# Second layer of a decoder step: keys' transposes a chunk later, values' products of four units in one visit, sums of squares later

## The chip, the cores and the metric

The kernel runs on one core of a Trainium2 chip. The metric is the device time of one execution in microseconds (us). The core has five engines with a queue each: TensorE (PE, matrix products and transposes; its loading of weights is shown apart as PEld), VectorE (DVE), ScalarE (ACT), GpSimd (POOL) and SyncE (SP, which mostly issues DMAs). An engine works through its queue in order; semaphores order the engines among each other.

## The reference

A decoder step of two layers for 1024 prompt tokens and 8 decode tokens, model width 1024. The first layer (retention) is untouched here. The second is attention in a sliding window with 16 query heads, 2 key and value heads, 64 elements a head:

```python
h = rmsnorm(x, g_norm)
q, k, v, gate = jnp.split(h @ w_in, [...], axis=-1)
q = rmsnorm(q.reshape(...), q_gain)              # over the 64 elements of a head
k = rmsnorm(k.reshape(...), k_gain)
# prompt: a block of 128 queries reads its own and the previous block of keys
scores = einsum('bnqkgd,bnskd->bnkgqs', qb, kk) * HD ** -0.5 - slope * dist   # masked
p = softmax(concat([scores, sink]))[..., :-1]
o = einsum('bnkgqs,bnskd->bnqkgd', p, vv)
# decode tokens: the same over the cached 128 keys and values and their own
return x + (o * silu(gate)) @ w_out, k[:, -128:], v[:, -128:]
```

## The kernel before

The text is about the second layer only, which runs from about 885 us to the end. Activations (`A_hi`, `A_lo`) and weights (`wh`, `wl`) are held as a rounded part and a remainder, and a product is made as three: hi·hi, lo·hi and hi·lo. Tokens lie in nine chunks c: eight of 128 prompt tokens and one of the 8 decode tokens; the projections take them in three groups ti of 384, 384 and 264 tokens.

**Keys and values.** A loop over n, 0 to 8. `kv_mm(n, 0)` and `kv_mm(n, 1)` are 12 products each of 256 columns (L1339 to L1341; the decode tokens' are L1336 and L1337). The PSUM tile comes from pool `pjp` (tiles `pj`) for even n and from `scp` (tiles `sc`, two banks) for odd n. `kv_ev` then has ACT write the values `vv` (L1346) and square the keys (L1312, tile `kj`, sums in `kss`), DVE scale the sums (L1313), POOL take the power −1/2 (L115, `krk`), DVE multiply by the token's factor (L1319) and write the normed keys `kd` (L1321). `kv_tr` transposes `kd` on TensorE (L100, `tr`); `kv_kk` splits the transposed keys into `kkh` (ACT, L1365) and `kkl` (DVE, L1366). Between them stand `rbcast`, three products with the unit matrix on DVE (L1396, tile `sq`), and `rbcast_mm`, a product with ones on TensorE (L1403, into an `sc` bank) that ACT copies to `rbc` (L1404): this brings the tokens' factors to all partitions for the gates. `q_conv` and `g_conv` split weights on ACT (L1102) and POOL (L1103) in the same loop. In this block (`sk`) TensorE, ACT, DVE, POOL and SP all keep the written order.

**Projections of queries and gates.** A generator (`pair_proj`, pairs p of heads 0 to 7) makes six tiles a pair: q for the three groups, and the gates g. A tile is 8 steps k of three products (L1132 to L1134). `q_ev` squares on ACT (L1450) and splits the queries; `ms_mm` sums the squares over a head with small products (L1471, L1473), and gives DVE and POOL the factor `rq`. The table `mms` says after which step k of which tile this stands. The generator runs at most four groups ahead of the scores and three ahead of the outputs.

**Units.** A unit is a pair p and a chunk c, 64 in all. `att_s` makes its scores (L1562, L1563, into an `sc` bank), DVE scales them and adds the bias (L1565), takes the maximum (L1567), ACT the exponential (L1569); `att_r` divides (DVE L1576, POOL L1577); `att_x` transposes the four quarters (L100) and ACT copies them to `ptf` (L1587); `att_o` multiplies by the values (L1600, 4 products, 2 for c = 0), ACT takes the result out (L1602), POOL multiplies by the gate (L1603). The main loop m gives, for each unit, the scores of m + 4, projections, the transposes of m + 1, projections, and the values' products of m; `fill(ps, W)` pulls projections of about 0.95 us. From m = 59 on the output projection fills in (`so_all`, generator `out`); `so_ahead` loads its weights and splits them (ACT L1119, DVE or POOL L1122). The decode tokens' scores (`dec_scores`, L1635 and L1640 on TensorE, L1623 to L1645 mostly on DVE) stand at m = 58.

In the main loop TensorE alone keeps the written order; the other engines' orders are set by the scheduler.

Of the kernel before, what the change touches and what calls it, by code (L numbers as in the profile page):

```python
# [7 lines left out]
F32 = mybir.dt.float32  # L8
# [62 lines left out]
def _trunk(ctx, tc, nc, a):  # L71
# [20 lines left out]
    mm = nc.tensor.matmul  # L92
# [501 lines left out]
    o = lambda fn, *a: (fn, a)  # L594
# [25 lines left out]
    n = 0  # L620
# [647 lines left out]
    o = 0  # L1268
# [58 lines left out]
    def kv_mm(c, h):  # L1327

        if h == 0:
            kvst[c] = (pjp.tile([128, 512], F32, tag="pj", name="pj") if c % 2 == 0 else  # L1330
                       scp.tile([128, 512], F32, tag="sc", name="sc"))
        ps = kvst[c]
        cs = slice(c * 128, c * 128 + 128)
        for k in range(4 * h, 4 * h + 4):
            if c == 8:
                mm(ps[0:40, :256], xdec2[:, k, :], kvs[0][:, k, :], start=(k == 0), stop=False)  # L1336
                mm(ps[0:40, :256], xdec2[:, k, :], kvs[1][:, k, :], start=False, stop=(k == 7))  # L1337
            else:
# [15 lines left out]
    def kv_tr(c):  # L1354
        kd = kvst.pop(c)
        pt = kvst["t", c] = trp.tile([128, 512], F32, name="tr")
        for g in range(2):
            tr(pt[:, g * 128:g * 128 + 128], kd[:, g].rearrange("p a b -> p (a b)"), ident)
        if c == 7:
            nc.scalar.dma_start(out=nkp[0, 0], in_=kd[:, :, 0, :])  # L1360

    def kv_kk(c):
        cs = slice(c * 128, c * 128 + 128)
        pt = kvst.pop(("t", c))[:, 0:256].rearrange("p (g t) -> p g t", g=2)
        nc.scalar.activation(kkh[:, :, cs], pt, AF.Copy)  # L1365
        nc.vector.tensor_tensor(kkl[:, :, cs], pt, kkh.bitcast(F32)[:, :, cs], ALU.subtract)  # L1366
# [20 lines left out]
    def rbcast(ti):  # L1387
        t0, t1 = TG[ti]
        n = t1 - t0
        dg = io("sq", 2)  # L1390
        if ti == 2:
            nc.gpsimd.memset(dg[:, 256:264], 0.0)
        for i in range(3):
            c = t0 // 128 + i
            m = 128 if c < 8 else ND
            nc.vector.tensor_scalar(dg[:m, i * 128:i * 128 + m], ident[:m, :m], r9[:m, c:c + 1], None, ALU.mult)  # L1396
        return dg

    def rbcast_mm(ti, dg):
        t0, t1 = TG[ti]  # L1400
        n = t1 - t0
        ps = scp.tile([128, 512], F32, tag="sc", name="sc")
        mm(ps[:, :n], ones, dg[:, :n], start=True, stop=True)  # L1403
        nc.scalar.activation(rbc[:, t0:t1], ps[:, :n], AF.Copy)  # L1404
# [29 lines left out]
    def pair_proj(p):  # L1434
# [64 lines left out]
            G[p, ti] = gt  # L1499

        order = ("q0", "q1", "g0", "q2", "g1", "g2") if p == 7 else ("q0", "q1", "q2", "g0", "g1", "g2")
        mms = {(1, 3): 0, (2, 3): 1, (4 if p == 7 else 3, 3): 2}
        for step, (kind, ti) in enumerate(order):
            ti = int(ti)
            isq = kind == "q"
# [73 lines left out]
    def att_x(u):  # L1579
        hs = (0, 1) if u.c > 0 else (1,)  # L1580
        pt = trp.tile([128, 512], F32, name="tr")
        for hf in hs:
            for j in range(2):
                tr(pt[:, hf * 256 + j * 128:hf * 256 + j * 128 + 128], u.st[:, j, hf * 128:hf * 128 + 128], ident)
        a0 = hs[0] * 256
        ptf = u.pt = atp.tile([128, 512], F32, name="ptf", bufs=2)
        nc.scalar.activation(ptf[:, a0:], pt[:, a0:], AF.Copy)  # L1587

    def att_o(u):
        p, ti, i, c = u.p, u.ti, u.i, u.c  # L1590
        if i == 0:
            ots[p, ti] = atp.tile([128, 384], F32, name="ot", bufs=2)
        ot, gt = ots[p, ti], G[p, ti]
        hs = (0, 1) if c > 0 else (1,)
        po = opp.tile([128, 128], F32, tag="o", name="o")
        vs = slice(u.g * 64, u.g * 64 + 64)
        for hf in hs:
            for j in range(2):
                rs_ = slice(hf * 256 + j * 128, hf * 256 + j * 128 + 128)
                mm(po[j * 64:j * 64 + 64, :], vv[:, c - 1 + hf, vs], u.pt[:, rs_], start=(hf == hs[0]), stop=(hf == 1))  # L1600
        cs = slice(i * 128, i * 128 + 128)
        nc.scalar.activation(ot[:, cs], po, AF.Copy, scale=0.5)  # L1602
        nc.gpsimd.tensor_tensor(ot[:, cs], ot[:, cs], gt[:, cs], ALU.mult)  # L1603
# [188 lines left out]
    def until(d, key):  # L1792
        while key not in d:
            next(ps)
# [7 lines left out]
    dgs = {}  # L1802
    for n in range(9):
        kv_mm(n, 0)
        if n == 2:
            rstd9(1)
        if n >= 2:
            kv_tr(n - 2)
        if 5 <= n < 8:
            rbcast_mm(n - 5, dgs.pop(n - 5))  # L1810
        kv_mm(n, 1)
        if n >= 3:
            kv_kk(n - 3)
        if n >= 1:
            kv_ev(n - 1)
        if 4 <= n < 7:
            dgs[n - 4] = rbcast(n - 4)
        if 1 <= n <= 4:
            q_conv(n - 1)
        if n == 3:  # L1820
            slots["g"], g_load, g_conv = wslot_parts(w_in_swa[:, 1280:1536])
            g_load(0)
        if n == 5:
            g_load(1)
        if 5 <= n <= 8:
            g_conv(n - 5)
    dec_load()
    fill(ps, 2.0)
    kv_kk(6)
    kv_dec()  # L1830
    kv_tr(7)
# [22 lines left out]
    fill(ps, 3.0)  # L1854
    att_r(units[3])
    att_x(units[0])
    sk.close()
    src = ps

# [4 lines left out]
            att_s(u)  # L1864
            att_r(u)

    for m in range(NU):
        u = units[m]
        if m == 50:
            lo_eng[0] = nc.vector  # L1870
            so_ahead(1)
        if m == 56:
            drain(ps)
            so_ahead(2)
        if m == 59:
            so_ahead(3)
            src = out
        reloads(m)
        sc_(m + L)
        if m == 58:  # L1880
            dec_scores()
            dec_vload()
        fill(src, W)
        if m + 1 < NU:
            att_x(units[m + 1])
        if m == 62:
            dec_pt()
        fill(src, W)
        until(G, (u.p, u.ti))
        att_o(u)  # L1890
        reloads(m)
        if m == 63:
            dec_o()
        fill(src, W)
    reloads(NU)
    drain(out)

# [37 lines left out]
```

## Time and profile before

| | |
|---|---|
| time of three runs, median (lowest to highest) | 1350.39 us (1350.27 to 1351.85) |
| the profiled execution | 1350.44 us, span 1348.6 us |
| mean granted clock of TensorE | 0.995 |
| busy: PE, DVE, ACT, POOL | 1308.8, 701.1, 633.6, 707.4 us |
| keys and values stage | 888.9 to 928.8 us, transposes of chunk 7 at 931.5 |
| steady loop over the units | about 1020 to 1225 us |
| scores of units 60 to 63 | from 1226.4 to 1235.2 us |

A row of a timeline reads: start, duration, engine, line of the kernel, operation, output tile <- input tiles, shape, how many records it joins, and in brackets the idle time of that engine just before, with what ended it. Buffer numbers are left out of names. One product of 32-bit numbers leaves two records in some shapes. A window gives the busy time of each engine in it and the granted clock of TensorE (1.00 is full).

### The profile page before, as it was taken

How to read it: one execution, taken by the hardware profiler on the slowest of the kernel's cores; microseconds unless marked ns; L12 is line 12 of the kernel's file. 1: busy time of each engine (PE TensorE's matmuls, PEld its weight loads, DVE VectorE, ACT ScalarE, POOL GpSimd, SP SyncE). 2: the span in 40 equal slices, each digit the busy share in tenths (PEclk: the TensorE clock that was granted, in tenths of full speed). 3: DMA queues.
4: the chain of work that ended last, by engine and by line, in shares of the span. 5: the costliest groups of instructions: out<-in, count | busy, mean ns of one | idle time of the engine just before them, and what ended most of it. 6: DMA issues, size and time to landing. Idle time of an engine off the chain costs nothing.

```text
span 1348.6 us, 25951 instructions
## 1 busy us (share of the span) xinstructions
PE 1308.8 (97%) x9661; PEld 1222.4 (91%) x9661; DVE 701.1 (52%) x1365; ACT 633.6 (47%) x1565; POOL 707.4 (52%) x825
## 2 busy tenths in 40 slices
PE   6999999999999999899999999998999999999998
PEld 6999999999999999787877899997889999998998
DVE  6943655656566553676752113335456555669321
ACT  5532444544455553677751112235465656656321
POOL 6653534435435543698977545454375666555000
PEclk9999999999999999999999999999999999999999
DMA  6314777587676753556556434442121111113532
GB/s 221 103 55 140 218 222 225 161 242 233 187 237 187 233 177 107 169 171 212 182 160 196 153 121 136 143 119 72 38 62 44 48 46 46 34 34 107 159 86 80
DMA packets 194771, 187.68 MB, mean 139 GB/s; under 512 B 12645, under 2 KB 174493, under 8 KB 194629
## 3 DMA queue, kind: packets, MB, share of 16 engines
q1 hardware_dynamic: 156576, 147.29, 35.9%
q10 hardware_dynamic: 38068, 38.73, 9.1%
q8 instruction: 76, 1.25, 0.4%
q14 instruction: 51, 0.41, 0.1%
HBM read 129.61 MB, written 57.41 MB: 139 GB/s over the span
## 4 chain that ended last, share of the span: by engine, by line
PE 85%; DVE 5%; POOL 4%; issue 3%; DMA 2%; ACT 1%; ACTq 0%; SPq 0%; POOLq 0%; DVEq 0%
PE b L330 7%; PE b L332 7%; PE b L331 7%; PE pj L1132 7%; PE pj L1134 6%; PE pj L1133 6%; PE b L323 4%; PE b L324 4%; PE b L325 4%; PE tr L100 4%; PE pj L1181 4%; PE pj L1179 4%; PE pj L1180 4%; PE o L1600 2%; POOL wl L1122 1%
## 5 line engine op out<-in xcount | busy, mean ns | idle before, releaser
L330 PE MATMUL b<-xh,woh 128*128 128x258 f32 x784 | 223.3, 285 | 0.0
L332 PE MATMUL b<-xh,wol 128*128 128x258 f32 x784 | 221.6, 283 | 0.0
L331 PE MATMUL b<-xl,woh 128*128 128x258 f32 x784 | 221.2, 282 | 0.0
L1132 PE MATMUL pj<-A_hi,wh 128*128 128x384 f32 (+1 forms) x512 | 178.7, 349 | 0.0
L1134 PE MATMUL pj<-A_hi,wl 128*128 128x384 f32 (+1 forms) x512 | 165.2, 323 | 0.0
L1133 PE MATMUL pj<-A_lo,wh 128*128 128x384 f32 (+1 forms) x512 | 165.1, 323 | 0.0
L330 PEld LDWEIGHTS b<-xh,woh 128*128 128x128 f32 x784 | 148.0, 189 | 4.1 <-issue 2.5
L331 PEld LDWEIGHTS b<-xl,woh 128*128 128x128 f32 x784 | 148.8, 190 | 0.0
L332 PEld LDWEIGHTS b<-xh,wol 128*128 128x128 f32 x784 | 148.1, 189 | 0.0
L221 POOL TENSOR_TENSOR wol<-raw,woh 128x512 fp32r<-128x512 f32 x52 | 68.5, 1325 | 139.7 <-ACT woh L216 139.0
L1122 POOL TENSOR_TENSOR wl<-wr,wh 128x1024 fp32r<-128x1024 f32 (+1 forms) x60 | 114.2, 1913 | 40.2 <-DVE wh L1121 19.5
L324 PE MATMUL b<-wol,xh 128*128 128x256 f32 x448 | 126.1, 281 | 0.3 <-DVE wol L221 0.3
L323 PE MATMUL b<-woh,xh 128*128 128x256 f32 x448 | 126.3, 282 | 0.0
L325 PE MATMUL b<-woh,xl 128*128 128x256 f32 x448 | 125.7, 281 | 0.0
L1132 PEld LDWEIGHTS pj<-A_hi,wh 128*128 128x128 f32 x512 | 97.3, 190 | 10.1 <-issue 9.4
L1133 PEld LDWEIGHTS pj<-A_lo,wh 128*128 128x128 f32 x512 | 97.6, 191 | 0.0
L1134 PEld LDWEIGHTS pj<-A_hi,wl 128*128 128x128 f32 x512 | 97.0, 190 | 0.0
L1577 POOL TENSOR_TENSOR s<-s,sm 128x512 f32<-128x512 f32 x64 | 68.9, 1077 | 49.7 <-DVE sm L1576 47.8
L323 PEld LDWEIGHTS b<-woh,xh 128*128 128x128 f32 x448 | 84.4, 188 | 2.5 <-issue 1.2
L324 PEld LDWEIGHTS b<-wol,xh 128*128 128x128 f32 x448 | 84.3, 188 | 0.8 <-DVE wol L221 0.8
L325 PEld LDWEIGHTS b<-woh,xl 128*128 128x128 f32 x448 | 84.3, 188 | 0.0
L1569 ACT ACTIVATE s<-s,mx 128x257 f32<-128x257 f32 x128 | 64.3, 505 | 30.2 <-DVE mx L1567 26.4
(379 smaller groups left out, 3564.7 us busy)
## 6 DMA issues: line engine op xcount, KB each, us to landing
raw<-in_w_in_ret_dram ACTq DMA_DIRECT2D x44, 512.0 KB
st<-in_state_ret_dram SPq DMA_DIRECT2D x64, 256.0 KB
out_dram<-st SPq DMA_DIRECT2D x64, 256.0 KB
wr<-in_w_out_ret_dram SPq DMA_DIRECT2D x32, 512.0 KB
wr<-in_w_in_swa_dram SPq DMA_DIRECT2D x18, 512.0 KB
vb<-vscr SPq DMA_DIRECT2D x64, 128.0 KB
evp<-qks SPq DMA_DIRECT2D x32, 256.0 KB
evx<-vsc SPq DMA_DIRECT2D x32, 256.0 KB
```

The costliest lines, as they stand in the source:

```text
L221: eng.tensor_tensor(lo, src_of(s, name, sub), hi.bitcast(F32), SUB)
L323: mm(dst, xh, wh, start=a and i == 0, stop=False, skip_group_check=True)
L324: mm(dst, xh, wl, start=False, stop=False, skip_group_check=True)
L325: mm(dst, xl, wh, start=False, stop=z, skip_group_check=True)
L330: mm(dst, wh, xh, start=a, stop=False, **sg)
L331: mm(dst, wh, xl, start=False, stop=False, **sg)
L332: mm(dst, wl, xh, start=False, stop=z, **sg)
L1122: lo_eng[0].tensor_tensor(lo[:, js, :], raw[:, i:i + step, :], hi.bitcast(F32)[:, js, :], ALU.subtract)
L1132: mm(ps, hi[:, k, fs], xh[:, k, t0:t1], start=first and k == ks[0], stop=False)
L1133: mm(ps, hi[:, k, fs], xl[:, k, t0:t1], start=False, stop=False)
L1134: mm(ps, lo[:, k, fs], xh[:, k, t0:t1], start=False, stop=last and k == ks[-1])
L1577: nc.gpsimd.tensor_tensor(st[:, :, 0:256], st[:, :, 0:256], sm.unsqueeze(2).broadcast_to([128, 2, 256]), ALU.mult)
```

## The change

In the stage of keys and values, `kv_tr` comes at n − 3 (n − 2 before) and `kv_kk` at n − 4 (n − 3); the first `rbcast` and its product move to n = 0 and 1 (4 and 5 before), the other two to 4, 5 and 5, 6 (5, 6 and 6, 7). The sums of squares stand after the seventh step of the next tile (fourth before). The values' products of four units are given in one visit into one PSUM tile, whose parts are taken out one after the other; six buffers of `ptf` (two before) hold the transposed quarters until then. The main loop runs over two units at a time, and the stretch of its end is written anew: the output projection is let in from m = 58.

```diff
-        mms = {(1, 3): 0, (2, 3): 1, (4 if p == 7 else 3, 3): 2}
+        mms = {(1, 6): 0, (2, 6): 1, (4 if p == 7 else 3, 6): 2}
...
-        ptf = u.pt = atp.tile([128, 512], F32, name="ptf", bufs=2)
+        ptf = u.pt = atp.tile([128, 512], F32, name="ptf", bufs=6)
...
-    def att_o(u):
-        p, ti, i, c = u.p, u.ti, u.i, u.c
+    def att_o(us):
+        po = opp.tile([128, 4, 128], F32, tag="o", name="o")
+        for n_, u in enumerate(us):
+            vs = slice(u.g * 64, u.g * 64 + 64)
+            hs = (0, 1) if u.c > 0 else (1,)
+            for hf in hs:
+                for j in range(2):
+                    rs_ = slice(hf * 256 + j * 128, hf * 256 + j * 128 + 128)
+                    mm(po[j * 64:j * 64 + 64, n_, :], vv[:, u.c - 1 + hf, vs], u.pt[:, rs_],
+                       start=(n_ == 0 and hf == hs[0]), stop=(hf == 1), skip_group_check=(n_ > 0))
+        for n_, u in enumerate(us):
+            att_out(u, po[:, n_, :])
+
+    def att_out(u, po):
...
         kv_mm(n, 0)
+        if n == 1:
+            rbcast_mm(0, dgs.pop(0))
         if n == 2:
             rstd9(1)
-        if n >= 2:
-            kv_tr(n - 2)
-        if 5 <= n < 8:
-            rbcast_mm(n - 5, dgs.pop(n - 5))
+        if n >= 3:
+            kv_tr(n - 3)
+        if n in (5, 6):
+            rbcast_mm(n - 4, dgs.pop(n - 4))
         kv_mm(n, 1)
-        if n >= 3:
-            kv_kk(n - 3)
+        if n >= 4:
+            kv_kk(n - 4)
+        if n == 0:
+            dgs[0] = rbcast(0)
+        if n in (4, 5):
+            dgs[n - 3] = rbcast(n - 3)
         if n >= 1:
             kv_ev(n - 1)
-        if 4 <= n < 7:
-            dgs[n - 4] = rbcast(n - 4)
...
+    kv_tr(6)
     fill(ps, 2.0)
+    kv_kk(5)
     kv_kk(6)
...
     att_x(units[0])
+    att_x(units[1])
...
-    for m in range(NU):
-        u = units[m]
+    for m in range(0, NU, 2):
...
-        if m == 59:
+        if m == 58:
             so_ahead(3)
             src = out
...
         fill(src, W)
-        if m + 1 < NU:
-            att_x(units[m + 1])
+        sc_(m + L + 1)
+        fill(src, W)
+        if m % 4 == 2:
+            us = units[m - 2:m + 2]
+            for u in us:
+                until(G, (u.p, u.ti))
+            att_o(us)
+        fill(src, 2 * W)
+        for n_ in (2, 3):
+            if m + n_ < NU:
+                att_x(units[m + n_])
+            if m == 62 and n_ == 3:
+                dec_pt()
+            fill(src, W)
+        reloads(m)
         if m == 62:
-            dec_pt()
-        fill(src, W)
-        until(G, (u.p, u.ti))
-        att_o(u)
-        reloads(m)
-        if m == 63:
             dec_o()
-        fill(src, W)
```

In the new kernel the values' products are line L1597, and what follows in the file has numbers six higher (the decode scores are L1641 and L1646, their copies L1642).

In three places the order of an engine's queue shows the change. The first is DVE's queue around chunk 3 of the keys (numbers tell the tiles apart; `kd` from an `sc` tile is that of an odd chunk). Before:

```order
L1321 SCALAR_TENSOR_TENSOR kd_11478<-pj_11386,krk_11473,kgb_11255 128x128 x2
L1366 TENSOR_TENSOR kkl_11289<-tr_11453,kkh_11288 128x2x128
L1313 TENSOR_SCALAR kss_11520<-kss_11520 128x2
L1319 TENSOR_SCALAR krk_11521<-krk_11521,r9_74 128x2
L1321 SCALAR_TENSOR_TENSOR kd_11526<-sc_11440,krk_11521,kgb_11255 128x128 x2
L1396 TENSOR_SCALAR sq_11530<-ident_69,r9_74 128x128 x3
L1366 TENSOR_TENSOR kkl_11289<-tr_11501,kkh_11288 128x2x128
```

And now:

```order
L1321 SCALAR_TENSOR_TENSOR kd_11480<-pj_11393,krk_11475,kgb_11255 128x128 x2
L1366 TENSOR_TENSOR kkl_11289<-tr_11457,kkh_11288 128x2x128
L1396 TENSOR_SCALAR sq_11520<-ident_69,r9_74 128x128 x3
L1313 TENSOR_SCALAR kss_11526<-kss_11526 128x2
L1319 TENSOR_SCALAR krk_11527<-krk_11527,r9_74 128x2
L1321 SCALAR_TENSOR_TENSOR kd_11532<-sc_11444,krk_11527,kgb_11255 128x128 x2
L1366 TENSOR_TENSOR kkl_11289<-tr_11503,kkh_11288 128x2x128
```

The diagonal (L1396) stands ahead of the keys of chunk 3 where it stood behind them, and it belongs to the second of the three broadcasts instead of the first.

The second is TensorE's queue at a visit to the values' products in the loop over the units, with the projections (L1132 to L1134) around it. Before:

```order
L1132 MATMUL pj_12143<-A_hi_7394,wh_11314 128x384
L1133 MATMUL pj_12143<-A_lo_7395,wh_11314 128x384
L1134 MATMUL pj_12143<-A_hi_7394,wl_11315 128x384
L1600 MATMUL o_12150<-ptf_12087,vv_11290 64x128 x4
L1132 MATMUL pj_12143<-A_hi_7394,wh_11314 128x384
```

And now:

```order
L1134 MATMUL pj_12215<-A_hi_7394,wl_11315 128x264
L1597 MATMUL o_12225<-ptf_12061,vv_11290 64x128 x2
L1597 MATMUL o_12225<-ptf_12068,vv_11290 64x128 x4
L1597 MATMUL o_12225<-ptf_12142,vv_11290 64x128 x4
L1597 MATMUL o_12225<-ptf_12155,vv_11290 64x128 x4
L1132 MATMUL pj_12215<-A_hi_7394,wh_11314 128x264
L1133 MATMUL pj_12215<-A_lo_7395,wh_11314 128x264
```

One visit with one `ptf` has become one with four, into one tile `o`; the first of these units has c = 0 and two products.

The third is DVE's queue in the tail, up to its first work on the decode scores. Before (`sc_15434` and `sc_15464` are units 61 and 62, `sc_15487` the first decode product):

```order
L1565 SCALAR_TENSOR_TENSOR s_15435<-sc_15434,rq_15126,ndp_14880 128x256
L1567 TENSOR_REDUCE mx_15407<-s_15406 128x2
L1565 SCALAR_TENSOR_TENSOR s_15435<-sc_15434,rq_15126,ndp_15132 128x256
L1565 SCALAR_TENSOR_TENSOR s_15465<-sc_15464,rq_15293,ndp_14880 128x256
L1567 TENSOR_REDUCE mx_15436<-s_15435 128x2
L1576 RECIPROCAL sm_15408<-sm_15408 128x2
L1565 SCALAR_TENSOR_TENSOR s_15465<-sc_15464,rq_15293,ndp_15132 128x256
L1636 TENSOR_TENSOR rbc_11293<-sc_15487,r16_11269 16x4x128
```

And now, from behind the scaling of unit 61 (`sc_15430` and `sc_15453` are unit 62 and the first decode product):

```order
L1576 RECIPROCAL sm_15373<-sm_15373 128x2
L1567 TENSOR_REDUCE mx_15388<-s_15387 128x2
L1122 TENSOR_TENSOR wl_15417<-wr_15418,wh_15416 128x512
L1122 TENSOR_TENSOR wl_15417<-wr_15424,wh_15416 128x512 x2
L1576 RECIPROCAL sm_15389<-sm_15389 128x2
L1565 SCALAR_TENSOR_TENSOR s_15431<-sc_15430,rq_15311,ndp_14836 128x256
L1565 SCALAR_TENSOR_TENSOR s_15431<-sc_15430,rq_15311,ndp_15087 128x256
L1630 TENSOR_TENSOR r16_11269<-r16_11269,rbc_11293 16x8
L1567 TENSOR_REDUCE mx_15432<-s_15431 128x2
L1631 TENSOR_SCALAR r16_11269<-r16_11269 16x8
L1633 TENSOR_TENSOR r16_11269<-r16_11269,rbc_11293 16x8
L1642 TENSOR_TENSOR rbc_11293<-sc_15453,r16_11269 16x4x128
```

Three splits of weights (L1122) stand ahead of unit 62 here, a fourth in the row before these, and the factor of the decode queries (`r16`) is worked out behind unit 62 instead of ahead of it.

More of the change, by code (lines that the diff above doesn't have):

```diff
@@ L1585, in att_x @@
         a0 = hs[0] * 256
-        ptf = u.pt = atp.tile([128, 512], F32, name="ptf", bufs=2)
+        ptf = u.pt = atp.tile([128, 512], F32, name="ptf", bufs=6)
         nc.scalar.activation(ptf[:, a0:], pt[:, a0:], AF.Copy)
-    def att_o(u):
-        p, ti, i, c = u.p, u.ti, u.i, u.c
+    def att_o(us):
[11 more added lines that the diff above has]
+    def att_out(u, po):
+        p, ti, i = u.p, u.ti, u.i
         if i == 0:
@@ L1593, in att_o @@
         ot, gt = ots[p, ti], G[p, ti]
[L1594 to L1600, printed above, removed]
         cs = slice(i * 128, i * 128 + 128)
```

## The prediction

> **What bounds the kernel now.** I read the busy shares first, then the windows of the second layer (885 us to the end), then TensorE's own rows at each place where a window is not full, and last the chain of waits.
>
> ```profile
> PE 1308.8 (97%) x9661; PEld 1222.4 (91%) x9661; DVE 701.1 (52%) x1365; ACT 633.6 (47%) x1565; POOL 707.4 (52%) x825
> 885.00:930.00 45.00, 38.03 (x279) 34.91 (x278) 20.82 (x53) 17.43 (x62) 18.96 (x24) 0.96 0.24 70
> 930.00:960.00 30.00, 27.45 (x176) 26.57 (x175) 14.68 (x39) 14.45 (x39) 13.68 (x20) 0.94 0.28 90
> 1020.00:1225.00 205.00, 205.00 (x1552) 187.96 (x1551) 127.22 (x281) 125.52 (x361) 122.11 (x176) 1.00 0.14 43
> 1225.00:1236.00 11.00, 10.20 (x98) 8.67 (x97) 10.96 (x26) 7.91 (x25) 5.78 (x9) 1.00 0.33 100
> ```
>
> A window row gives its length, then the busy time of PE, PEld, DVE, ACT and POOL, then the granted clock. TensorE sets the pace. From 1020 to 1225 it is busy all of 205 us while DVE, ACT and POOL stand at 122 to 127, so in that loop only time taken from TensorE itself counts. TensorE waits in three places: 45 − 38.03 = 7.0 us in the keys and values stage, 30 − 27.45 = 2.55 us in the next window, and 1.5 us near 1010 (its row comes below). In the tail (1225 to 1236) DVE is full, 10.96 of 11 us, and TensorE has almost no slack to it.
>
> **Keys and values one step deeper.** The waits of this stage stand ahead of the transposes of the keys (L100).
>
> ```profile
> 914.54 0.59 PE L100 MATMUL tr<-ident,kd 128*128 128x128 f32 x2 [1.72 <-DVE kd L1321]
> 915.47 0.88 PE L1403 MATMUL sc<-sq,ones 128*128 128x384 f32 x2 [0.35 <-DVE sq L1396]
> 920.94 0.59 PE L100 MATMUL tr<-ident,kd 128*128 128x128 f32 x2 [1.76 <-DVE kd L1321]
> 927.48 0.59 PE L100 MATMUL tr<-ident,kd 128*128 128x128 f32 x2 [1.18 <-DVE kd L1321]
> 931.46 0.38 PE L100 MATMUL tr<-ident,kd 128*128 128x128 f32 x2
> ...
> 910.03 0.49 ACT L1404 ACTIVATE rbc<-sc 128x384 f32<-128x384 f32 x1 [4.59 <-PE sc L1403]
> ...
> 905.06 0.41 DVE L1366 TENSOR_TENSOR kkl<-tr,kkh 128x256 fp32r<-128x256 f32 x1
> 905.39 0.16 DVE L1313 TENSOR_SCALAR kss<-kss 128x2 f32<-128x2 f32 x1
> 906.36 1.25 DVE L1319 TENSOR_SCALAR krk<-krk,r 128x2 f32<-128x2 f32 x1 [0.81 <-POOL krk L115]
> 907.71 0.61 DVE L1321 SCALAR_TENSOR_TENSOR kd<-sc,krk,kgb 128x128 f32<-128x128 f32 x2
> 908.24 0.67 DVE L1396 TENSOR_SCALAR sq<-ident,r 128x128 f32<-128x128 f32 x3
> ```
>
> The transposes of chunks 4 to 6 come 914.54, 920.94, 927.48, a step of 6.4 to 6.5 us, while the 24 products of a chunk need about 2.9 (a pitch of 0.119). Around chunk 5 the loop is closed: the broadcast product L1403 waits for DVE's diagonal (L1396), ACT stands 4.59 us at its copy L1404 with the squares of the next chunk queued behind it, and those feed DVE's kd, for which the next transpose waits. The change opens the loop: the first broadcast goes to chunk 1, and the transposes run a chunk later. What is left is the chain on DVE: kkl 0.41, kss 0.16, the wait for POOL 0.81, krk 1.25, kd 0.61, which adds to 3.24 us a chunk, and 0.67 more where a diagonal stands ahead.
>
> So I set the stage by that chain, from kd of chunk 0. It ends about 1 us later than before, since ACT now has the copy L1404 (0.49) and four DMA issues in front of the squares of chunk 0. kd of chunk 3 then ends near 910.4 (908.3 before: 1.2 from the start, 0.67 for the diagonal that now stands ahead of it, the rest kkl). The second broadcast product, at chunk 5, takes the PSUM bank of chunk 3 and so waits for exactly this kd. TensorE is there at 907.25: a new wait of 3.2 us, with all products of chunk 5 behind it. After it I have a wait of 2.05 us at the transposes of chunk 6 and 0.35 at chunk 7. New waits are 5.6 in all, old ones 7.0: 1.4 us. The slow stretch that follows the wait at 920.94 goes too (next fence: 3.78 us of work at a clock of 0.66, so 3.78 × 0.34 = 1.3 us), and five restarts fewer, at about 0.2 each (a transpose takes 0.59 after a wait and 0.38 without): 1.0. Together **−3.7 us**. Bounds: nothing saved (the chain as slow as before), and −6.6 (nearly all waits gone).
>
> A wait can cost clock afterwards.
>
> ```profile
> 920.00:925.00 5.00, 3.78 (x15) 3.30 (x16) 2.15 (x8) 1.91 (x8) 0.40 (x1) 0.66 0.37 105
> 950.00:955.00 5.00, 5.00 (x24) 4.54 (x24) 2.27 (x8) 0.91 (x4) 2.14 (x3) 0.77 0.53 164
> 948.29 0.61 PE L1471 MATMUL pm<-C,sq 128*128 128x2 f32 x4 [2.55 <-ACT sq L1450]
> 948.95 0.69 PE L1132 MATMUL pj<-A_hi,wh 128*128 128x384 f32 x1
> 951.67 0.52 PE L1134 MATMUL pj<-A_hi,wl 128*128 128x384 f32 x1
> 1119.40 0.33 PE L1134 MATMUL pj<-A_hi,wl 128*128 128x384 f32 x1
> ```
>
> After the 1.76 us wait at 920.94 the granted clock of the stretch is 0.66, after the 2.55 us wait 0.77. In the latter the nine products from 948.95 to 951.67 run at a pitch of 0.34 us instead of 0.175 (0.340 × 9 − 0.175 × 9 = 1.5 us). I charge one such spell, **+1.5 us**, to the new 3.2 us wait; the ends are 0 and 1.7.
>
> [...]
>
> **Sums of squares later.** The products L1471 go from the fourth to the seventh k of the next tile, 9 products later. Before, the third one waited 2.55 us for ACT (row at 948.29), whose square sat behind the exponentials of two units and a copy. By the new order TensorE gets there near 942.6 and the square is done at 940.4, because three more groups of products lie between. The wait and the cold spell behind it go: **−4.1 us**. The wait at 1011 is of the same kind, and goes too: **−1.5 us**.
>
> ```profile
> 1011.03 0.83 PE L1471 MATMUL pm<-C,sq 128*128 128x2 f32 x6 [1.52 <-ACT sq L1450]
> ```
>
> What is later is rq (DVE, POOL), by 1.6 us; scores are asked for four units ahead, so nothing waits. Ends: 0 and −5.6 for both.
>
> **Values' products of four units in one visit.** A visit of TensorE to the small products and back:
>
> ```profile
> 1114.77 0.33 PE L1134 MATMUL pj<-A_hi,wl 128*128 128x384 f32 x1
> 1115.04 0.44 PE L1600 MATMUL o<-ptf,vv 128*64 128x128 f32 x4
> 1115.41 0.44 PE L1132 MATMUL pj<-A_hi,wh 128*128 128x384 f32 x1
> 1115.69 0.34 PE L1133 MATMUL pj<-A_lo,wh 128*128 128x384 f32 x1
> ...
> 1119.66 0.66 PE L1600 MATMUL o<-ptf,vv 128*64 128x128 f32 x8
> 1120.25 0.44 PE L1132 MATMUL pj<-A_hi,wh 128*128 128x384 f32 x1
> 1120.53 0.34 PE L1133 MATMUL pj<-A_lo,wh 128*128 128x384 f32 x1
> ...
> L1602 ACT ACTIVATE ot<-o 128x128 f32<-128x128 f32 x44 | 11.8, 268 | 0.9 <-PE o L1600 0.7
> L1603 POOL TENSOR_TENSOR ot<-ot,gt 128x128 f32<-128x128 f32 x44 | 23.6, 535 | 19.5 <-ACT ot L1602 19.5
> ```
>
> A projection is followed by the next after 0.175. With 8 records between, the times from 1119.40 to 1120.53 are 1.13, less two projections 0.35: 0.78 us. With 4 records, 1114.77 to 1115.69 is 0.92, less 0.35: 0.57. So a record costs (0.78 − 0.57) / 4 = 0.053, and a visit 0.35 whatever it holds: late entry, the way back, one slow first projection. 64 visits become 16; 48 × 0.34 = **−16.3 us**. The ends: 0 if the price hangs on the change of unit rather than on the way in and out, and −16.6. In the steady loop nothing covers this, TensorE being full there. Against it stands that outputs come in bursts of four (ACT 4 × 0.27, POOL 4 × 0.54); the window has 44 units, 4.66 us each, so four units are 18.6 us; each engine has over 70 us of slack in 205, and the scores stand at least two units (9 us) ahead of their transposes, so I cost the burst at nothing. If a visit comes too early for the last ptf, it waits for ACT (the second rival).
>
> **The tail.** Here order changes on a full DVE.
>
> ```profile
> 1227.76 0.91 DVE L1496 SCALAR_TENSOR_TENSOR gt<-gt,sq 128x264 f32<-128x264 f32 x1
> 1229.06 0.47 DVE L1565 SCALAR_TENSOR_TENSOR s<-sc,rq,ndp 128x256 f32<-128x256 f32 x1
> 1229.45 0.67 DVE L1567 TENSOR_REDUCE mx<-s 128x2 f32<-128x514 f32 x1
> 1230.57 1.06 PE L1635 MATMUL sc<-acc,Qd 128*16 128x128 f32 x8 [0.42 <-DVE s L1565]
> 1232.01 1.06 PE L1635 MATMUL sc<-acc,Qd 128*16 128x128 f32 x8 [0.38 <-DVE s L1565]
> 1219.81 0.68 DVE L1122 TENSOR_TENSOR wl<-wr,wh 128x512 fp32r<-128x512 f32 x1
> 1222.76 2.08 POOL L115 TENSOR_TENSOR r<-r,mhalf 16x8 f32<-16x8 f32 x1
> 1257.41 0.48 PE L1677 MATMUL o<-pm,vdd 8*128 8x128 f32 x2 [0.38 <-ACT ot L1602]
> ```
>
> Scores of units 60, 61 and 62 now come in 2.3 us of TensorE's time, and the decode tokens' scores right behind; two PSUM banks serve all of them. Each of the two decode products waits until DVE has read the unit before. Unit 61: DVE owes unit 60 (2 × 0.47), a gate (0.91), a maximum (0.67) and unit 61 (2 × 0.47), 3.5 us, from the end of the scores of 60, TensorE has 2.1 to do, so about 1.4 us. Unit 62: four splits L1122 (4 × 0.68) now stand ahead of it on DVE, and one maximum 0.67; some run while TensorE still does the first decode product, 2.7 us (4.0 if none does). Scores of 63 wait until DVE has read the first decode product, which needs r: the 2.08 us of POOL's power now come after unit 62, 1.6 us. The output projection starts sooner against its data: 0.8 for A_hi, 1.9 for A_lo of the last heads. Together 8.4 us; old waits 0.42 + 0.38 + 0.38 go, and a cold spell more than before comes (1.5): **+8.5 us** in round numbers. Ends: +2 (only the waits for units 61 and 62, half as long) and +13 (no split early, two cold spells).
>
> **Sum.** −3.7 + 1.5 − 4.1 − 1.5 − 16.3 + 8.5 = −15.6. The profiled execution took 1350.44 us (span 1348.6), 0.05 above the median of the three runs, 1350.39; I forecast **1334.8 us**, 1.2% faster. About 0.2%, 2.7 us, is what can be told from no change.
>
> **Rivals.**
> 1. The tail loses nothing: DVE catches up while TensorE is in the output projection. For it: in 1225 to 1236 the same DVE work fitted with only 0.8 us of waiting. Against: four splits are now written ahead of unit 62, and TensorE has less to do in between. 1334.8 − 8.5 = 1326.3.
> 2. Slower: each visit waits for the ptf of its last unit. In half of the visits only two units' scores (0.93 us) lie between the last transposes and the visit. If ACT, at that moment, is in an exponential pair and the copy (1.2 us with the queue), 16 visits × 1.2 = 19.2 and the time is 1354.0. It decides from 1.0 us a visit on (15.6 / 16). Against: TensorE gives its projections ahead of most transposes, and ACT has 80 us free in 205.
> 3. The fixed price belongs to a unit, not to a visit: the 16.3 go, 1351.1, no change. For it: each unit brings its own weights ptf. Against: 4 records and 8 records give one line, and a visit of 8 already changes its weights.
> 4. The stage of keys and values gains nothing, its DVE chain being the bound, or the tail takes its upper end: 1334.8 + 3.7 = 1338.5, or + 4.5 = 1339.3, or both, 1343.0.
>
> **Chances.** The forecast 0.60 (its own range 1329 to 1338), the tail without loss 0.16, the stage or tail worse 0.15, no change by the unit price 0.05, slower 0.04. Faster by over 0.2% is the first three, 0.91; within 0.2% 0.05; slower 0.04. The range, 1324 to 1345, holds the first three with their bounds.
>
> **What would show it.** Right: between 905 and 913 a wait of about 3 us of L1403 for kd; no wait of L1471 over 0.3 us; rows of 28 to 32 records of the values' products (L1597) taking about 1.8 us, and 2 us less for each pair of heads (6 visits × 0.34); the decode scores (L1641) waiting 1 to 4 us for DVE. Wrong: L1597 waiting for ptf in each visit, records further apart than 0.06 us, or DVE's wl ahead of unit 62 waiting for its DMA, which would stretch the tail beyond 13 us.

## The result, and the profile after

The changed kernel took 1341.73 us (median of four runs, 1338.14 to 1342.46), the kernel before 1350.33 beside it: a ratio of 0.9929, 95% interval 0.9916 to 0.9941, so 8 to 11 us less. The forecast was 1334.8 in a range of 1324 to 1345. The profiled execution took 1341.06, 9.4 less than the profiled one of before; 15.6 were forecast. One execution of one kernel below (the four-unit visits alone) took 2546 us and is left out of all figures.

The page of the changed kernel has TensorE busy for 11.9 us less (1308.8 before) at the same share of the span:

```profile
PE 1296.9 (97%) x9661; PEld 1226.6 (92%) x9661; DVE 693.8 (52%) x1365; ACT 629.8 (47%) x1565; POOL 705.6 (53%) x825
```

The waits view of TensorE over the second layer gives who was waited for, the time in all, how often, and the longest (rows of over 1 us):

```profile
PE sc L1641 <- DVE s L1565: 4.6, 2, 2.5
PE pj L1132 <- ACT A_hi L1617: 2.7, 1, 2.7
PE sc L1403 <- DVE kd L1321: 2.6, 1, 2.6
PE pm L1471 <- ACT sq L1450: 1.9, 1, 1.9
PE tr L100 <- DVE kkl L1366: 1.7, 1, 1.7
PE pj L1133 <- DVE A_lo L1618: 1.1, 1, 1.1
```

Five of the six had been forecast; the wait of the sums of squares (L1471) was to have gone. The timeline of TensorE shows where they lie:

```profile
910.46 0.88 PE L1403 MATMUL sc<-sq,ones 128*128 128x384 f32 x2 [2.60 <-DVE kd L1321]
923.06 0.44 PE L100 MATMUL tr<-ident,kd 128*128 128x128 f32 x2 [1.65 <-DVE kkl L1366]
1007.52 0.83 PE L1471 MATMUL pm<-C,sq 128*128 128x2 f32 x6 [1.87 <-ACT sq L1450]
1210.02 1.89 PE L1641 MATMUL sc<-acc,Qd 128*16 128x128 f32 x8 [2.06 <-DVE s L1565]
1214.41 1.89 PE L1641 MATMUL sc<-acc,Qd 128*16 128x128 f32 x8 [2.50 <-DVE s L1565]
1227.38 0.69 PE L1132 MATMUL pj<-A_hi,wh 128*128 128x384 f32 x1 [2.74 <-ACT A_hi L1617]
1229.21 0.69 PE L1133 MATMUL pj<-A_lo,wh 128*128 128x384 f32 x1 [1.14 <-DVE A_lo L1618]
```

The windows of the same execution (length, then busy PE, PEld, DVE, ACT, POOL, then the granted clock) show what the waits of the tail cost beyond themselves:

```profile
885.00:930.00 45.00, 40.62 (x314) 39.00 (x314) 23.28 (x62) 19.44 (x69) 21.79 (x28) 1.00 0.30 88
1010.00:1015.00 5.00, 5.00 (x25) 4.97 (x26) 3.87 (x11) 3.45 (x12) 3.18 (x3) 0.79 0.00 0
1210.00:1215.00 5.00, 2.48 (x11) 1.45 (x12) 5.00 (x11) 2.41 (x8) 2.07 (x2) 0.51 0.22 63
1215.00:1220.00 5.00, 5.00 (x35) 4.62 (x33) 2.05 (x8) 1.94 (x5) 2.66 (x2) 0.50 0.37 124
1230.00:1235.00 5.00, 5.00 (x22) 4.89 (x21) 4.11 (x6) 1.93 (x3) 0.05 (x1) 0.60 0.21 57
1255.00:1260.00 5.00, 5.00 (x23) 4.96 (x23) 2.17 (x6) 2.13 (x7) 0.00 (x0) 0.72 0.43 131
```

From 1210 to 1220 TensorE has half its clock, and 0.60 again from 1230. Busy time times (1 − clock), added over all windows of 5 us in the second layer, is 4.4 us in the kernel before and 9.4 in the changed one.

And a visit of four units, in the row of 32 records and the projection behind it:

```profile
1017.54 0.28 PE L1563 MATMUL sc<-kkl,qs 128*128 128x256 f32 x1
1017.75 1.97 PE L1597 MATMUL o<-ptf,vv 128*64 128x128 f32 x32
1019.65 0.44 PE L1132 MATMUL pj<-A_hi,wh 128*128 128x384 f32 x1
```

The 32 records and the way back take 1.90 us, where four visits of eight took four times 0.59.

To see where the time went I compare the first score product of the same unit in both traces (both by the start of the layer's first product, L1339, at 888.92 before and 889.60 now). At unit 1 the changed kernel is 4.3 us ahead, at unit 2 8.6, at unit 24 14.5, at unit 56 22.2. From 24 to 56, four whole pairs of heads, it gains 7.8. At unit 60 it is 21.5 ahead, at the end only 10.3: the tail gives back 11.3 us.

### The profile page after: what moved, and what is told of

Same layout as the page of the kernel before. It is cut to its first block, busy times and chain, and to the rows that moved or that the text cites. A ratio compares the mean times of both kernels' runs of the same rounds, so it can differ in the third digit from the quotient of the medians.

```text
span 1339.0 us, 25986 instructions
## 1 busy us (share of the span) xinstructions
PE 1296.9 (97%) x9661; PEld 1226.6 (92%) x9661; DVE 693.8 (52%) x1365; ACT 629.8 (47%) x1565; POOL 705.6 (53%) x825
## 4 chain that ended last, share of the span: by engine, by line
PE 84%; DVE 5%; POOL 4%; issue 2%; ACT 2%; DMA 2%; ACTq 0%; SPq 0%; POOLq 0%; DVEq 0%
PE b L330 7%; PE b L332 7%; PE b L331 7%; PE pj L1132 6%; PE pj L1133 5%; PE pj L1134 5%; PE b L323 4%; PE b L324 4%; PE b L325 4%; PE tr L100 4%; PE pj L1181 4%; PE pj L1179 4%; PE pj L1180 4%; PE o L1597 2%; POOL wl L1122 1%
## 5 line engine op out<-in xcount | busy, mean ns | idle before, releaser
L1132 PE MATMUL pj<-A_hi,wh 128*128 128x384 f32 (+1 forms) x512 | 176.6, 345 | 2.9 <-ACT A_hi L1617 2.7
L1134 PE MATMUL pj<-A_hi,wl 128*128 128x384 f32 (+1 forms) x512 | 166.0, 324 | 0.0
L221 POOL TENSOR_TENSOR wol<-raw,woh 128x512 fp32r<-128x512 f32 x52 | 68.4, 1324 | 139.3 <-ACT woh L216 127.8
L1122 POOL TENSOR_TENSOR wl<-wr,wh 128x1024 fp32r<-128x1024 f32 (+1 forms) x60 | 114.0, 1911 | 38.2 <-DVE wh L1121 19.2
L1132 PEld LDWEIGHTS pj<-A_hi,wh 128*128 128x128 f32 x512 | 98.3, 192 | 6.7 <-ACT A_hi L1617 3.1
L1134 PEld LDWEIGHTS pj<-A_hi,wl 128*128 128x128 f32 x512 | 97.8, 191 | 0.0
```

The lines of the kernel that those rows point to most:

```text
L221: eng.tensor_tensor(lo, src_of(s, name, sub), hi.bitcast(F32), SUB)
L1122: lo_eng[0].tensor_tensor(lo[:, js, :], raw[:, i:i + step, :], hi.bitcast(F32)[:, js, :], ALU.subtract)
L1132: mm(ps, hi[:, k, fs], xh[:, k, t0:t1], start=first and k == ks[0], stop=False)
L1134: mm(ps, lo[:, k, fs], xh[:, k, t0:t1], start=False, stop=last and k == ks[-1])
```

## The experiments

Twelve kernels were run, each with its runs beside runs of the kernel before on the same chip.

**One part alone: the stage of keys and values.** The loop over n of the changed kernel in the kernel before.

> The kernel before with the stage of keys and values of the changed kernel alone (transposes a chunk later, the first broadcast at chunk 1); the rest is that of before. Theory (the trace of the changed kernel, where the transposes of chunk 7 end 5.9 us sooner by the layer's own start): 5 to 6 us less than before, about 1344.8, with one wait of some 2.6 us of the broadcast product L1403. The prediction's term (3.7 less, 1.5 of it given back to a cold clock): 1348.2. Rival: the chain on DVE bounds the stage whatever the order, and what is saved here is waited for at the sums of squares near 945, whose wait of 2.55 us grows: 1350, no change.

Measured: 1346.91, ratio 0.9969 (0.9954 to 0.9984): 2 to 6 us less. The wait is there, 2.61 us, and in this profiled execution, the fastest of the ten (1344.11), no slow stretch came behind it (clock 1.00 from 910 to 925). By the medians the gain, 3.4 us, lies between the two forecasts. The wait at the sums of squares is 2.68, so nothing of the gain was waited for there. The stage's gain is real, and of the three parts it is the only one that pays on its own.

**One part alone: the sums of squares.**

```diff
-        mms = {(1, 3): 0, (2, 3): 1, (4 if p == 7 else 3, 3): 2}
+        mms = {(1, 6): 0, (2, 6): 1, (4 if p == 7 else 3, 6): 2}
```

> The kernel before with the sums of squares after the seventh step alone. Theory: the wait of 2.55 us near 948 and the slow stretch behind it go, 4 us less (1346.3); the wait of 1.5 us near 1011 does not go, since in the changed kernel it is still there (1.87 us) and comes from ACT standing at the issue of a DMA, not from the place of the product. Prediction: both go, 5.6 less (1344.8). Rival: rq comes later and the scores wait for it; no gain (1350).

Measured: 1351.12, ratio 1.0001 (0.9992 to 1.0011): no change. Both waits went, that at 1011 too, against my theory. But TensorE has a new one in the tail, and DVE's timeline says why:

```profile
1229.12 0.83 DVE L1624 TENSOR_TENSOR r<-r,rbc 16x8 f32<-16x8 f32 x1
1229.88 0.67 DVE L1122 TENSOR_TENSOR wl<-wr,wh 128x512 fp32r<-128x512 f32 x1
1231.15 0.14 DVE L1625 TENSOR_SCALAR r<-r 16x8 f32<-16x8 f32 x1
1234.41 0.15 DVE L1627 TENSOR_TENSOR r<-r,rbc 16x8 f32<-16x8 f32 x1 [2.53 <-POOL r L115]
1235.40 0.38 PE L1562 MATMUL sc<-kkh,qs 128*128 128x256 f32 x1 [3.42 <-DVE rbc L1636]
```

The decode tokens' factor r starts from the last pair's sum of squares. That sum now comes at 1218.24; in the next run, which differs in this alone, it comes at 1213.94. The factor's steps fell behind splits and maxima in DVE's queue, then behind a division on POOL; it was ready at 1234.6, in the kernel before at 1227.3 (L1627 in both traces). The scores of unit 63 waited 3.42 us.

**The same, with the last sum left where it was.**

```diff
-        mms = {(1, 6): 0, (2, 6): 1, (4 if p == 7 else 3, 6): 2}
+        mms = {(1, 6): 0, (2, 6): 1, (4, 3) if p == 7 else (3, 6): 2}
```

> The kernel before with the sums of squares after the seventh step, as in the second run, but for the last one of the last pair, which stays after the fourth. Theory: in the second run the gain ahead (the waits of 2.55 and 1.5 us) was lost in the tail, where the decode tokens' factor, which starts from this very sum, ended behind DVE's maximum and splits and the scores of unit 63 waited 3.42 us for it; with the sum back in its place that wait goes, the gain stays: 4 to 6 us less than before, 1345 to 1347. Rival (the wait comes from the scheduler's order of DVE as a whole, or the gain ahead was never there): 1350 to 1351, as in the second run.

Measured: 1347.58, ratio 0.9961 (0.9944 to 0.9978): 3 to 8 us less. The 3.42 us wait is gone. One entry of the table had cost what the others won.

**One part alone: the loop with four units in a visit**, with keys, values and sums of squares as before.

> The changed kernel with the stage of keys and values and the place of the sums of squares as before: the loop over two units with the products of four in a visit, alone. Theory (0.32 us a visit, 1.94 a pair of heads as read in the changed kernel, the tail as there): at the scores of unit 60 some 14 us less than before, and 9 to 11 of them lost in the tail: 1345 to 1347 in all. If the tail's loss comes for the larger part from the late sums of squares (rival): the tail loses 5 or less, 1340 to 1342.

Measured: 1356.81, ratio 1.0030 (1.0018 to 1.0043): slower than before by 2 to 6 us, outside both expectations. The visits do pay, 7.1 us from unit 24 to unit 56, or 1.77 a pair. But at the scores of unit 60 the lead is 6.0, where 14 were expected, and at the end nothing of it is left. This profiled execution, the slowest of the kernel (1359.23), lost 2.7 us before the layer began and 1.8 more by unit 0, with slow stretches from 915 to 935 (clock 0.79, 0.86 and 0.66 in the windows at 915, 920 and 930); up to there the work of the two kernels does not differ. Two losses belong to the change. The tail loses 11.7 us from unit 60 to the end, as in the changed kernel, so the late sums of squares are not its larger part. And near 1021, with slow stretches behind it (clock 0.53 and 0.78 from 1020 to 1030):

```profile
1021.21 1.44 PE L1471 MATMUL pm<-C,sq 128*128 128x2 f32 x6 [4.62 <-ACT sq L1450]
1015.24 0.44 ACT L1608 ACTIVATE ot<-o 128x128 f32<-128x128 f32 x2
1019.80 0.33 ACTq L1614 DMA_DIRECT2D oscr<-ot  x1
1020.18 0.60 ACT L1587 ACTIVATE ptf<-tr 128x512 f32<-128x512 f32 x1 [4.50 <-POOL ot L1609]
1020.67 0.48 ACT L1450 ACTIVATE sq<-pj 128x384 f32<-128x384 f32 x1
1015.93 1.28 POOL L1122 TENSOR_TENSOR wl<-wr,wh 128x512 fp32r<-128x512 f32 x1
1017.17 0.86 POOL L1609 TENSOR_TENSOR ot<-ot,gt 128x128 f32<-128x128 f32 x2
1018.00 1.35 POOL L115 TENSOR_TENSOR rq<-rq,mhalf 128x6 f32<-128x6 f32 x1
1019.32 0.45 POOL L1609 TENSOR_TENSOR ot<-ot,gt 128x128 f32<-128x128 f32 x1
```

ACT takes out the outputs in one go and comes to the DMA that stores them (L1614, in ACT's own queue). It stands there 4.5 us for the third gate on POOL, which has a split and a power ahead of it. The squares for the sums lie behind the DMA, and TensorE waits 4.62 us for them. Sums three steps later, as in the changed kernel, cover a part of this: 1.87 us is left.

**The outputs' DMA issued by SP.**

```diff
-                nc.scalar.dma_start(out=oscr[p, :, u.t0:u.t0 + n], in_=ot[:, :n])
+                nc.sync.dma_start(out=oscr[p, :, u.t0:u.t0 + n], in_=ot[:, :n])
```

> The changed kernel with the DMA that puts a pair's outputs into memory issued by SP instead of ACT. Theory: at 1006 ACT stands 3.35 us at this issue, waiting for POOL's third gate, with the square behind it that the sums of squares wait for; with the issue on SP this wait of 1.87 us and the slow stretch behind it (1.5 us) go: 3 us less, 1338.5. Rival: POOL's splits of weights hold up the gates and ACT's own copies as well, so that the wait stays: 1341.7. Rival on the other side: SP's queue holds back loads of weights behind the issue: slower, 1343 or more.

Measured: 1340.02, ratio 0.9916 (0.9889 to 0.9943). The wait of L1471 is gone. From unit 16 to unit 24 this kernel gains 1.7 us on the kernel before, where the changed one loses 2.0. Of these 3.7 us 1.7 are left at the end by the medians. In this execution 1.35 went to a slow stretch at 910 (clock 0.73) that the changed kernel's did not have, and the tail waits more: 3.63 us instead of 2.50 at the second decode product, and 2.20 anew at the decode tokens' output (L1683). The mechanism is shown, the whole time is not clear of the changed kernel's.

**Two units in a visit.**

```diff
-        if m % 4 == 2:
-            us = units[m - 2:m + 2]
+        if True:
+            us = units[m:m + 2]
```

> The changed kernel with the values' products of two units in a visit instead of four, at each step of the loop: 32 visits instead of 16. Theory (a fixed price of 0.34 us a visit, whatever it holds): 16 x 0.34 = 5.4 us more in the loop; the scores of unit 60 come 4.8 us later than in the changed kernel; the tail may win a part back, since the outputs of units 56 and 57 come sooner. Whole time 1341.7 + 5.4 = 1347, or less by what the tail wins. Rival (the price belongs to a unit or its weights): unit 60 comes at the same time, whole time 1341.7.

Measured: 1342.94, ratio 0.9937 (0.9916 to 0.9957). From unit 24 to unit 56, 4.8 us are won on the kernel before: 1.19 a pair for four visits fewer, 0.30 a visit. The changed kernel has 1.94 for six fewer, 0.32 a visit. Two visits of this stretch waited for ptf (0.85 and 0.62 us), which the 0.30 contains. The rows show the price without waits; here is a visit of 12 records in this run and one of 28 in the changed kernel:

```profile
1071.42 0.33 PE L1134 MATMUL pj<-A_hi,wl 128*128 128x384 f32 x1
1071.69 0.88 PE L1597 MATMUL o<-ptf,vv 128*64 128x128 f32 x12
1072.49 0.44 PE L1132 MATMUL pj<-A_hi,wh 128*128 128x384 f32 x1
1072.78 0.34 PE L1133 MATMUL pj<-A_lo,wh 128*128 128x384 f32 x1
...
1071.45 0.34 PE L1134 MATMUL pj<-A_hi,wl 128*128 128x384 f32 x1
1071.72 1.75 PE L1597 MATMUL o<-ptf,vv 128*64 128x128 f32 x28
1073.40 0.44 PE L1132 MATMUL pj<-A_hi,wh 128*128 128x384 f32 x1
1073.68 0.34 PE L1133 MATMUL pj<-A_lo,wh 128*128 128x384 f32 x1
```

From the first row's start to the last one's are 1.36 and 2.23 us; the visits of 4 and 8 records in the kernel before take 0.92 and 1.13. With 0.35 for two projections taken off, all four lie within 0.02 us of 0.34 a visit and 0.055 a record, whether the records are those of one unit, of two or of four. The price belongs to the visit. But unit 60 came 7.4 us later than in the changed kernel, more than the 4.8 expected: 0.75 a pair over seven and a half pairs is 5.6, and 1.5 were lost to a slow stretch at 910 (clock 0.66) that the changed kernel's execution did not have. At the end 1.2 are left by the spans, because the tail gives back 5.0 here and 11.3 there; that its outputs come by two is a likely reason, not shown alone.

**The tail: the third weights' split later.**

```diff
         if m == 58:
-            so_ahead(3)
             src = out
+        if m == 60:
+            so_ahead(3)
```

> The changed kernel with the third set of output weights loaded and split from m = 60 on instead of 58. Theory (DVE is what the tail waits for, and the four splits ahead of unit 62 are a part of it): the second decode product's wait of 2.5 us goes down by about 2 us, and the stretch at a clock of 0.51 to 0.76 behind it gets shorter; 2 to 4 us less, 1338 to 1340. Rival (the tail waits for the outputs of units 56 to 59, and time won ahead of that is waited for there): the wait for A_hi grows by as much, 1341.7.

Measured: 1337.47, ratio 0.9901 (0.9879 to 0.9923). The second decode product's wait went from 2.50 to 0.38, as expected. In its place the scores of unit 63 wait 3.35 us for L1642, the late decode factor of the second run, and the waits for A_hi and A_lo are 1.55 and 1.39. This profiled execution was the slowest of the four (1341.32).

**The tail: the products of units 56 to 59 ahead of the decode scores.**

```diff
+        if m == 58:
+            us = units[56:60]
+            att_o(us)
             dec_scores()
```

> The changed kernel with the values' products of units 56 to 59 given right after the scores of unit 62, ahead of the decode tokens' scores, instead of behind the scores of 63. Theory: ACT's copies, POOL's gates and the split A_hi, A_lo then run while TensorE has the decode scores and the first projections; the waits of 2.74 (A_hi) and 1.14 (A_lo) and a slow stretch of 1.5 us go: 4 to 5 us less, 1337. Rival: DVE stands at A_lo, which now lies ahead of the decode tokens' factor in its queue, and the scores of 63 wait for it: 1340 to 1343.

Measured: 1335.43, ratio 0.9888 (0.9859 to 0.9916), below the expected 1337. Both waits for A_hi and A_lo are gone; the second decode product waits 3.85.

**All three of these edits.**

> The changed kernel with all three: the outputs' DMA on SP, the third split at m = 60, the products of units 56 to 59 ahead of the decode scores. Theory: waits of 1.87, about 2, 2.74 and 1.14 us and two or three slow stretches of 1.5 us go: 9 to 12 us less than the changed kernel, 1330 to 1333. If the parts hide the same wait (rival): 1336 to 1338, no better than the best of them.

Measured: 1328.07, ratio 0.9831 (0.9807 to 0.9855), 13.7 below the changed kernel by the medians, 13.2 by the two ratios: more than expected. Of the tail's 8.4 us of waiting 1.9 are left (unit 62) and 1.0 at the decode tokens' output; the loss to the clock is down from 9.4 to 4.4. The parts did not hide the same wait; each fix alone had sent TensorE into the next one.

**The broadcasts a chunk later.**

```diff
-        if n in (5, 6):
-            rbcast_mm(n - 4, dgs.pop(n - 4))
+        if n in (6, 7):
+            rbcast_mm(n - 5, dgs.pop(n - 5))
...
-        if n in (4, 5):
-            dgs[n - 3] = rbcast(n - 3)
         if n >= 1:
             kv_ev(n - 1)
+        if n in (5, 6):
+            dgs[n - 4] = rbcast(n - 4)
```

> The changed kernel with the second and third broadcast a chunk later (products at chunks 6 and 7, DVE's diagonals behind the keys). Theory (the wait of 2.6 us at the broadcast product comes from the PSUM bank of chunk 3 and DVE's keys of it, but the DVE chain of 3.2 us a chunk bounds the stage): that wait goes, waits at the transposes come in its place, the end of the transposes of chunk 7 moves by 0 to -1.5 us: 1340.2 to 1341.7. Rival (the bank is all there is to it): 2.6 us less, 1339.1. On the other side: the loop of before closes again, 1343 or more.

Measured: 1343.67, ratio 0.9947 (0.9931 to 0.9964); the bound named for the other side. The wait for the keys became waits of 2.71 and 1.62 us for the diagonals (L1396), which now lie behind the keys on DVE. The transposes of chunk 7 come 3.4 us later than in the changed kernel by the layer's own start, where 0 to 1.5 sooner had been expected.

**A bank of their own for the broadcasts**, on top of the three edits.

```diff
-        ps = scp.tile([128, 512], F32, tag="sc", name="sc")
+        ps = msp.tile([128, 512], F32, tag="ms", name="pm")
         mm(ps[:, :n], ones, dg[:, :n], start=True, stop=True)
```

> The seventh run's kernel with the three broadcast products in a PSUM bank of their own (that of the sums of squares, free in this stage). Theory (the wait of 2.6 us comes from the bank of chunk 3, but DVE's chain of 3.2 us a chunk bounds the stage): the wait goes; waits at the transposes or the splits of the keys take up half of it or more; with the slow stretch behind it (1.5 us, seen in most runs) 1 to 3 us less, 1325 to 1327. Rival (the chain is all): 1328, no change. Rival (the bank is all): 4 us less, 1324.

Measured: 1325.69, ratio 0.9795 (0.9776 to 0.9814), 2.4 less than without by the medians. The two kernels ran on different chips and their intervals overlap, so the size is not clear. In the new trace the broadcast products wait for nothing, and the transposes of the last chunks for the splits:

```profile
908.06 0.81 PE L1403 MATMUL pm<-sq,ones 128*128 128x384 f32 x2
917.97 0.44 PE L100 MATMUL tr<-ident,kd 128*128 128x128 f32 x2 [0.19 <-DVE kkl L1366]
921.13 0.69 PE L100 MATMUL tr<-ident,kd 128*128 128x128 f32 x2 [1.78 <-DVE kkl L1366]
```

Of the 2.60 us 1.1 are won: the transposes of chunk 7 come 35.56 us after the layer's start, 36.63 in the changed kernel. TensorE's idle time up to there fell by 2.4, from 4.37 to 1.97; a slow stretch behind the wait of 1.78 (clock 0.66 from 920 to 925), which the changed kernel's execution did not have, took 1.3 back. What DVE's chain still holds up is 1.97 where 1.65 stood, so the bank is the larger part of the 2.60, larger than the theory had it.

**And the last pair's sum after the fourth step.**

> The same with the last pair's third sum of squares after the fourth step. Theory: the decode tokens' factor was already in time in the seventh run, so 0 to 1 us less than the run before this one. Rival: the sum waits for ACT there, as it did at 1011 before: 1.5 us more.

Measured: 1323.26, ratio 0.9786 (0.9758 to 0.9815), the fastest of all: 25 to 33 us below the kernel before. It is 2.4 below the run ahead of it by the medians, more than expected, but the runs of both overlap (1322.0 to 1327.7 against 1325.0 to 1326.8). TensorE's waits of over 0.3 us in the layer are down to these:

```profile
PE sc L1562 <- DVE s L1565: 3.2, 1, 3.2
PE tr L100 <- DVE kkl L1366: 2.0, 2, 1.8
```

## Why the prediction was right, and where it was off

The time fell inside the range, and most of the places it named were right. It did not fall into the 1329 to 1338 of the main case: 1341.7 lies where the fourth rival had put the stage or the tail at its worse end (1338.5 to 1343.0, a chance of 0.15), and the tail is what did it. In the order of the sum, with what the two profiled executions show:

| term | forecast | measured |
|---|---|---|
| keys and values, with its slow stretch | −3.7 + 1.5 | −5.9 |
| sums of squares at 945 | −4.1 | −4.3 |
| sums of squares at 1011 | −1.5 | +1.8 |
| visits | −16.3 | −15.5 |
| tail | +8.5 | +13.2 |
| start of the layer | 0 | +0.7 |
| sum | −15.6 | −10.0 |

Visits are 48 × 0.32, the price read from unit 24 to 56; the tail's 13.2 are the 11.3 given back and 1.9 for the six visits fewer among the last eight units, which the row of visits has. The span is 9.6 less, so 0.4 is not placed. The errors partly cancel: keys and values came out 3.7 better than forecast, the sums at 1011 and the tail 8.0 worse. Part of keeping inside the range is this luck.

- Keys and values: the transposes of chunk 7 come at 926.23, where 931.46 stood, 5.9 sooner by the layer's own start. The new wait at the broadcast product was forecast as 3.2 us at 910.45 and is 2.60 at 910.46; those of 2.05 and 0.35 at the last transposes are 1.65 and nothing. That the two times agree to 0.01 us is luck, as the layer began 0.7 later. From the layer's start to the transposes of chunk 7 TensorE's idle time fell from 6.96 to 4.37 us, 2.6 where 1.4 were forecast, and its busy time from 35.58 to 32.26, 3.3 where the slow stretch and the restarts were to give 2.3. What I charged for a new slow stretch did not come in this execution; in five others it did (last section).
- Sums of squares at 945: the wait and the slow stretch are gone, as worked out.
- Sums of squares at 1011: here a step failed. I took the wait for one of the same kind and let the later product cover it. The product is three steps later, but the four outputs taken out at once bring ACT to the DMA that waits for POOL's gates, with the squares behind it:

```profile
1006.12 0.33 ACTq L1614 DMA_DIRECT2D oscr<-ot  x1
1006.49 0.60 ACT L1587 ACTIVATE ptf<-tr 128x512 f32<-128x512 f32 x1 [3.35 <-POOL ot L1609]
1006.98 0.49 ACT L1450 ACTIVATE sq<-pj 128x384 f32<-128x384 f32 x1
```

  So 1.87 us stay where 1.52 were, and a slow stretch follows (1.4 us, the windows at 1005 and 1010, clock 0.87 and 0.79). The run with the DMA on SP shows the cause, and in the run with the late sums alone, without the burst, the wait went as forecast. I had costed the burst of outputs at nothing, by the slack of ACT and POOL over 205 us; it has a price where POOL splits weights in the same 5 us.
- Visits: the fixed price of 0.34 us is confirmed by the rows of visits of 4 to 28 records; the loop as a whole gained 0.32 for each visit fewer, and nothing in it waited for ptf. The rival of a price by unit is out; the rival of a wait in each visit did not occur. These products are 128 × 64 where the projections are 128 × 128 (rows above), and no run takes this change of shape away alone, so why a visit costs the 0.34 us is not shown.
- Tail: the waits add to 2.06 + 2.50 + 2.74 + 1.14 = 8.4 us, and 8.4 was forecast, though not in the same parts: unit 63 waited for nothing, and A_hi took 1.9 more, as the four gates came in one slow burst on POOL:

```profile
1223.25 3.93 POOL L1609 TENSOR_TENSOR ot<-ot,gt 128x128 f32<-128x128 f32 x4 [3.41 <-ACT ot L1608]
```

  The mis-sized term is the clock's share of the tail. I charged one more slow stretch, 1.5 us. The windows lose 8.0 us from 1210 on, and 1.7 in the same part of the kernel before: 6.3 more.
- That rq comes 1.6 us later and "nothing waits" was wrong as well: the decode factor hangs on the last sum, which came 4.3 us later in the second run than in the third, and the scores of unit 63 waited for it. In the changed kernel they did not: slowed down itself, TensorE reached them at 1218.81, after DVE had read the decode products (L1642, done at 1218.66).

Without a loss of clock the tail's four waits, 1.14 to 2.74 us, would have cost only themselves, and the time would have been about 6 us less, by an estimate from the windows (8.0 − 1.7). The windows at 0.50 and 0.60 show the loss. The prediction charged 1.5 us of clock to the new wait in the stage of keys and values and 1.5 more in its tail term, 3.0 in all. The wait of 2.60 us left the clock full here and was followed by a window of 0.66 in the run with the three edits; no run shows what decides between the two.

## What to carry to other kernels

When the engine that sets the pace is relieved, look at what it is ahead of next: the loop's 15 us came through to the whole time only with the tail and the order of a DMA made to fit, and each of those fixes alone moved the wait to the next consumer. A batch is not free for the engines behind it: its outputs come in a burst, and whatever waits in order behind the burst (here a DMA in ACT's queue, for 3.35 us) holds up work that has nothing to do with it. A wait of TensorE cost more than itself in some places of these runs: 1.87 us drew 1.4 more behind it, the tail's 8.4 drew 6.3, and in the run with two units in a visit 1.10 us of idle time drew 1.7 (5.00 us at a clock of 0.66). It is a chance and not a rule, for the 1.52 us at 1011 in the kernel before drew nothing.

## What the runs showed of the hardware

Some of TensorE's waits of 1.1 to 2.7 us in these runs were followed by a lower clock, down to 0.50 (the tail of the changed kernel), and others were not: behind the 1.65 us at 923.06 in the changed kernel the window from 925 to 930 has a clock of 1.00. For one and the same wait it changes from one profiled execution to another. In the changed kernel and in a kernel with the same stage (the three edits) the wait of 2.60 us at the broadcast is followed by these windows:

```profile
910.00:915.00 5.00, 4.54 (x33) 4.24 (x34) 2.28 (x8) 2.36 (x9) 1.58 (x2) 1.00 0.36 107
```

```profile
910.00:915.00 5.00, 4.12 (x18) 3.55 (x19) 1.74 (x8) 2.24 (x8) 0.61 (x1) 0.66 0.34 105
```

It was 0.66 to 0.73 in five of the seven profiled executions with this wait, and full in two. That is 1.4 us behind a single wait in the second row. The four runs of the changed kernel spread over 4.3 us, the fastest at a mean clock of 0.994 and the others at 0.989 to 0.990, so several such places can be what parts them. In the run with two units in a visit TensorE was idle for only 1.10 us from 1010 to 1015 (3.90 busy of 5.00), and the window from 1015 to 1020 has a clock of 0.66.

Small work on POOL stretched in the tail. A gate takes 0.46 us (the median of 64 in the changed kernel), and four in the tail took 3.93 together, the first 1.71 (row above). DVE was busy for 2.79 us of that time. What sets the stretch was not tried.
